# Second FFN cut into four groups with block steps in fourteen places, first queries projected ahead of the later values, sign changes tied to their places

## The chip, the core and the metric

The program runs on one NeuronCore of a Trainium2 chip. Its engines work side by side, each through its own list in order: TensorE (PE, the matrix engine; PEld is its loading of weights), VectorE (DVE), ScalarE (ACT), GpSimd (POOL) and SyncE (SP), which issues most of the transfers from device memory. PE writes into PSUM; DVE and ACT read it from there. The metric is the device time of one execution in microseconds (us), as the median of the runs. The times before were 1147.1, 1148.95 and 1351.8 us.

## The reference

Two trunk layers over 512 tokens of width 1024, batch 1. Layer 0 mixes by attention (with 256 context tokens), layer 1 by a Fourier transform and a linear map; both end with a gated feed-forward net (FFN) of width 2816 with a width-3 convolution. Every sub-layer stands between two RMS norms, with shift, scale and gate (adaLN) computed from the conditioning vector.

```python
for i in range(2):
    sh1, sc1, g1, sh2, sc2, g2 = split(silu(c) @ mod_w[i] + mod_b[i], 6)
    h = rms_norm(x, norm_g[i, 0]) * (1 + sc1) + sh1
    if i == 0:
        proj = h @ w_in                 # queries a, b, then keys and values a, b
        y = concat([global_attention(...), window_attention(...)]) @ w_out
    else:
        y = real(fft2(h.reshape(512, 4, 256), axes=(0, 2))) @ w_f
    x = x + g1 * rms_norm(y, norm_g[i, 1])
    h = rms_norm(x, norm_g[i, 2]) * (1 + sc2) + sh2
    u = h @ w_up                        # 1024 -> 2 x 2816
    u = up[:-2] * cw[0] + up[1:-1] * cw[1] + up[2:] * cw[2] + cb
    gate, val = split(u, 2)
    x = x + g2 * rms_norm((silu(gate) * val) @ w_down, norm_g[i, 3])
```

## The kernel before

All data stay transposed: 128 channels on the partitions, tokens along the row. An fp32 operand is split into a high part (fp32r) and the rest, and a product takes three matmuls: high by high (L98), one rest (L99) and the other (L100). For a weight, SP loads the raw fp32 tile (ring `raw`, three buffers), ACT casts the high part `wh`, DVE subtracts to get `wl` (both L121), and the pair stands in the ring `wpair` of five buffers.

An FFN runs over 22 chunks `fi` of 128 gate and 128 value channels. A plain up step takes 2 x 8 x 3 = 48 matmuls of 512 columns. A block step (`seven_products`; the chunks listed in `SEVEN`) computes the 2 x 2 blocks of the same product by seven block products: 7 x 4 x 3 = 84 matmuls of 256 columns. It needs four weight pairs of 1 MB in all instead of two, a second raw buffer filled by DVE sums (L1126, L1128, L1129), and two corrections of its outputs on DVE (L1168, L1171). After either step `conv` (ACT L1222, DVE L1223 and L1225, twice each) and `gated` (product L1236, split into a high and a low part, L121) follow.

The chunks are gathered in `GROUPS`, before (0 to 7), (8 to 13), (14 to 21). When the up steps of a group are through, its eight down tiles d = 0 to 7 follow: one raw tile each (512 KB for 8 chunks, 384 KB for 6), 3 matmuls per chunk, and from the second group on an addition to `yT` on DVE (L1343). The generator `gem` forms sums for the last adaLN vectors (raw loads of `mod_r`, L423 and L426 on DVE); `pump` advances a generator by one step. In the last group ACT loads a table early through `once` (L1358), so that the reciprocal square root of the norm (L186) finds it there.

In the attention part `project` runs for the groups of heads `kb` (keys), `vb` (values) and `qa` (queries), in that order, and the queries go through the norm on DVE, the rotation (to L773) and transposes on PE (L951). In the Fourier part `up_weights_dma` fetches the first pairs of the FFN without ACT casts or DVE rests: GpSimd's queue loads `xh`, ACT writes its negative into `xl` (L1093), and a second transfer adds the weight to `xl`. There, the loop over d = 0 to 7 multiplies by `w_f`; its weights are sums and differences (POOL and DVE), cast on ACT (L121) and split on DVE.

The order of instructions on each engine is set by the code's order and by a scheduler that sorts it with a planner's costs; each engine then runs its list strictly in order. The `later` and `held` marks shift single instructions in that list.

## Time and profile before

| | us |
|---|---|
| runs | 1147.1, 1148.95, 1351.8 (median 1148.95) |
| profiled execution, its time | 1146.93 |
| its span in the profile | 1145.2 |
| clock granted to PE, mean | 0.992 |
| attention start to end of layer 0, then Fourier part, FFN of layer 1 | 0 to about 690, 690 to 760, 760 to 1145 |

The profile lists, for one execution, each engine's busy time, the groups of instructions by source line, the transfers, and the chain of work that ended last. The table of stretches gives busy time within a stretch of the span; PEclk is the clock that PE was granted there, as a share of full speed. Stretches between 924.64 and 1075.02 us hold single up steps of layer 1 and serve as the price list below. Consecutive instructions on an engine overlap by some hundredths of a microsecond, so start times lie a little closer than the durations say.

### The profile page before, as it was taken

The numbers are of one execution on the slowest core, as the hardware profiler recorded it, in microseconds if no ns is written. First come the engines' busy times: TensorE is split into PE (matmuls) and PEld (weight loads), VectorE is DVE, ScalarE is ACT, GpSimd is POOL, SyncE is SP. The second block draws the span as 40 slices with busy tenths as digits, with TensorE's granted clock in tenths as the row PEclk, the third lists the DMA queues.
The fourth block names the chain that finished last, engine by engine and source line by source line (L and its number), as shares of the span: only waits on it lengthen the run. The fifth ranks groups of instructions, "written<-read, shape, count | busy, mean of one in ns | idle before, by whom it ended". The sixth has DMA issues, their size and how long they took to land.

```text
span 1145.2 us, 19120 instructions
## 1 busy us (share of the span) xinstructions
PE 1117.5 (98%) x7658; PEld 964.3 (84%) x7658; DVE 871.9 (76%) x1418; ACT 579.2 (51%) x1032; POOL 174.3 (15%) x180
## 2 busy tenths in 40 slices
PE   8999999999999999999999999999999999999996
PEld 5689988868898978987898898879887888899895
DVE  4678777765679976987999667878996498679745
ACT  4342356665665633552465545557743455256542
POOL 1136332421420000000000153510000000000012
PEclk9999999999999999999999999999999999999998
DMA  9576101075142355635534301920227223223212
GB/s 371 242 240 213 45 1 38 13 261 205 38 185 111 103 198 214 221 120 203 193 110 175 108 26 57 258 92 35 74 82 254 75 106 111 86 99 111 93 56 74
DMA packets 31745, 151.61 MB, mean 132 GB/s; under 512 B 3236, under 2 KB 7972, under 8 KB 19752
## 3 DMA queue, kind: packets, MB, share of 16 engines
q1 hardware_dynamic: 30504, 146.19, 36.0%
q0 software_dynamic: 1152, 4.19, 1.5%
q8 instruction: 60, 0.98, 0.3%
q14 instruction: 29, 0.24, 0.1%
HBM read 146.18 MB, written 4.19 MB: 131 GB/s over the span
## 4 chain that ended last, share of the span: by engine, by line
PE 89%; DVE 6%; ACT 4%; issue 1%; DMA 0%; POOL 0%; DVEq 0%; SPq 0%; ACTq 0%; POOLq 0%
PE mm L98 26%; PE mm L99 24%; PE mm L100 24%; PE PT L922 1%; ACT wh L121 1%; PE O L98 1%; PE gm L499 1%; PE gm L98 1%; PE O L99 1%; PE gm L100 1%; PE gm L99 1%; PE mm L174 1%; PE O L100 1%; PE mm L180 1%; DVE md_t L231 1%
## 5 line engine op out<-in xcount | busy, mean ns | idle before, releaser
L121 ACT CAST wh<-raw 128x1024 fp32r<-128x1024 f32 (+2 forms) x189 | 180.3, 966 | 186.6 <-PE mm L99 125.0
L121 DVE TENSOR_TENSOR wl<-raw,wh 128x1024 fp32r<-128x1024 f32 (+3 forms) x179 | 202.9, 1142 | 65.3 <-ACT wh L121 65.1
L98 PE MATMUL mm<-hh,wh 128*128 128x256 f32 (+2 forms) x652 | 221.0, 339 | 1.3 <-ACT yT L897 0.9
L99 PE MATMUL mm<-hl,wh 128*128 128x256 f32 (+2 forms) x652 | 218.2, 335 | 0.0
L100 PE MATMUL mm<-hh,wl 128*128 128x256 f32 (+2 forms) x652 | 217.9, 334 | 0.0
L273 POOL TENSOR_TENSOR gacc<-gacc,sq 128x256 f32<-128x256 f32 (+1 forms) x33 | 29.6, 897 | 717.6 <-ACT sq L271 716.9
L98 PEld LDWEIGHTS mm<-hh,wh 128*128 128x128 f32 x652 | 122.5, 188 | 18.6 <-ACT sq L1162 2.7
L100 PEld LDWEIGHTS mm<-hh,wl 128*128 128x128 f32 x652 | 122.6, 188 | 14.1
L99 PEld LDWEIGHTS mm<-hl,wh 128*128 128x128 f32 x652 | 122.6, 188 | 13.8
L98 PE MATMUL mm<-xh,wh 128*128 128x512 f32 (+1 forms) x368 | 131.6, 358 | 0.0
L99 PE MATMUL mm<-xl,wh 128*128 128x512 f32 (+1 forms) x368 | 131.1, 356 | 0.0
L100 PE MATMUL mm<-xh,wl 128*128 128x512 f32 (+1 forms) x368 | 130.1, 354 | 0.0
L98 PE MATMUL mm<-zh,wh 128*128 128x256 f32 x304 | 86.5, 285 | 0.0
L99 PE MATMUL mm<-zl,wh 128*128 128x256 f32 x304 | 84.3, 277 | 0.0
L100 PE MATMUL mm<-zh,wl 128*128 128x256 f32 x304 | 84.3, 277 | 0.0
L98 PEld LDWEIGHTS mm<-xh,wh 128*128 128x128 f32 x368 | 69.1, 188 | 12.8 <-issue 2.1
L99 PEld LDWEIGHTS mm<-xl,wh 128*128 128x128 f32 x368 | 69.1, 188 | 11.3 <-issue 0.4
L100 PEld LDWEIGHTS mm<-xh,wl 128*128 128x128 f32 x368 | 69.0, 188 | 11.1
L1222 ACT ACTIVATE cv<-mm,cols 128x512 f32<-128x512 f32 x64 | 49.7, 776 | 28.1 <-PE mm L100 25.0
L98 PEld LDWEIGHTS mm<-zh,wh 128*128 128x128 f32 x304 | 57.2, 188 | 3.6 <-ACT sq L1165 2.8
L1223 DVE SCALAR_TENSOR_TENSOR cv<-mm,cols,cv 128x511 f32<-128x511 f32 x64 | 47.5, 744 | 12.9 <-ACT cv L1222 12.4
L99 PEld LDWEIGHTS mm<-zl,wh 128*128 128x128 f32 x304 | 57.2, 188 | 0.0
(426 smaller groups left out, 2681.7 us busy)
## 6 DMA issues: line engine op xcount, KB each, us to landing
raw<-in_w_up SPq DMA_DIRECT2D x42, 1024.0 KB, 4.9
xT<-in_mod_r SPq DMA_DIRECT2D x20, 1024.0 KB, 4.9
raw<-in_w_down SPq DMA_DIRECT2D x32, 512.0 KB, 3.8
raw<-in_mod_p SPq DMA_DIRECT2D x8, 1024.0 KB, 5.0
raw<-in_w_in SPq DMA_DIRECT2D x6, 1024.0 KB, 8.0
raw<-in_w_down SPq DMA_DIRECT2D x16, 384.0 KB, 3.1
yT<-in_mod_r SPq DMA_DIRECT2D x10, 512.0 KB, 6.7
raw<-in_w_out SPq DMA_DIRECT2D x4, 1024.0 KB, 5.0
```

The lines of the kernel that those rows point to most:

```text
L98: i = PE.matmul(out, lhsT=ah, rhs=bh, start=start, stop=False, skip_group_check=skip)
L99: PE.matmul(out, lhsT=ah, rhs=bl, start=False, stop=False, skip_group_check=skip)
L100: return i, PE.matmul(out, lhsT=al, rhs=bh, start=False, stop=stop, skip_group_check=skip)
L121: i = S.copy(out=h, in_=src), eng.tensor_tensor(out=l, in0=src, in1=f(h), op=ALU.subtract)
L174: PE.matmul(ps[:32, :src.shape[1]], lhsT=ones32, rhs=src, start=True, stop=True)
L180: PE.matmul(ps[32 * j:32 * j + 32, :w], lhsT=ones32, rhs=sq[:, j * w:(j + 1) * w], start=first, stop=last)
L231: V.scalar_tensor_tensor(out=t, in0=src, scalar=am, in1=R, op0=ALU.mult, op1=ALU.mult)
L273: G.tensor_tensor(out=self.acc[:, sl], in0=self.acc[:, sl], in1=sq[:, sl], op=ALU.add)
L499: PE.matmul(ps[32 * q:32 * q + 32, :], lhsT=spad[:, k, :], rhs=w[:, q * T:(q + 1) * T], start=k == 0, stop=k == KC - 1)
L922: PE.transpose(out=pt[:, j * P:(j + 1) * P], in_=Ps[j][:, off:off + P], identity=ident)
L1222: S.activation(out=cv, in_=ps, func=AF.Identity, bias=bc, scale=wc[1])
L1223: V.scalar_tensor_tensor(out=cv[:, 1:], in0=ps[:, :T - 1], scalar=wc[0], in1=cv[:, 1:], op0=ALU.mult, op1=ALU.add)
```

## The change

1. The groups of layer 1 become (0 to 3), (4 to 9), (10 to 15), (16 to 21), and all of 8 to 21 are block steps (before, nine of them: 10, 13, 16, 19 and 21 were plain). The down tiles of a finished group no longer run in one piece: they are taken one or two at a time (four after 8 and 9) between the up steps of the next group, by the table `DOWN`. `gem` is advanced after down tiles 1, 4 and 7 of the middle groups, where it stood behind every tile of group 0. With the finer groups there are 32 down tiles for 24; the matmuls are as many.
2. The residual `xT` is stored to device memory (`away`, 2 MB) and its buffer holds gate pairs of chunks 0 to 3 and 10 to 13; it is loaded again in the last group, ahead of the weights of d = 6 and 7.
3. The early table load through `once` is removed in both layers. ACT's list now has the table load directly ahead of the reciprocal square root.
4. The attention projects `kb`, `qa`, `vb` instead of `kb`, `vb`, `qa`; the keys' and values' preparations for the first head stand behind the last `vb`, the inverse roots of the second half of the queries are put off by `later`, and the second job of `gate` has two buffers instead of all.
5. `up_weights_dma` issues its four sign changes one by one at d = 3, 4, 5 and 6 (before: all four by the pump at d = 4), each tied behind the last ACT instruction in the list. Two Fourier buffers move within `yT` for it.

```diff
-GROUPS = [(0, 8), (8, 6), (14, 8)]
+GROUPS = [[(0, 8), (8, 6), (14, 8)], [(0, 4), (4, 6), (10, 6), (16, 6)]]
...
-SEVEN = [(5, 6, 8, 10, 12, 14, 15, 17, 18, 20), (8, 9, 11, 12, 14, 15, 17, 18, 20)]
+SEVEN = [(5, 6, 8, 10, 12, 14, 15, 17, 18, 20), (8, 9, 10, 11, 12, 13, 14, 15, 16, 17, 18, 19, 20, 21)]
+DOWN = {8: 4, 9: 4, 10: 1, 11: 1, 12: 1, 13: 2, 14: 1, 15: 2, 16: 1, 17: 1, 18: 1, 19: 2, 20: 1, 21: 2}
...
-            for g, kind in enumerate(["kb", "vb", "qa"]):
+            for g, kind in ((0, "kb"), (2, "qa"), (1, "vb")):
...
-        for (wh, wl), src in ws:
-            S.activation(out=wl, in_=f(wh), func=AF.Copy, scale=-1.0)
-        yield
-        for (wh, wl), src in ws:
-            G.dma_start(out=wl, in_=src, accum_op=ALU.add)
+        for i, ((wh, wl), src) in enumerate(ws):
+            if i:
+                G.dma_start(out=ws[i - 1][0][1], in_=ws[i - 1][1], accum_op=ALU.add)
+            last = [j.name for j in nc.cur_bb.bb.instructions if j.engine == mybir.EngineType.Activation][-1]
+            j = S.activation(out=wl, in_=f(wh), func=AF.Copy, scale=-1.0)
+            tc.add_manual_dep(j.ins, last, mybir.DependencyInfo(
+                mybir.DependencyClass.NoSync, mybir.DependencyReason.DATA), reason="order")
+            yield
+        G.dma_start(out=wl, in_=src, accum_op=ALU.add)
...
-                gs["t"] = xp.pair([P, 2, T])
+                gs["t"] = places.pop(0) if l and (f0 == 0 or f0 == 10 and fi < 14) else xp.pair([P, 2, T])
...
+        def down_tiles(gi, nch, g_):
+            yield
+            for d in range(KC):
+                down_part(gi, down_weights(gi, nch, d, wpair), g_, d, [0, 1])
+
+                if gi and d % 3 == 1:
+                    pump(gem)
+                yield
...
+            SY.dma_start(out=away, in_=xT)
...
+                if l:
+                    pump(down, DOWN.get(fi, 0))
+            pump(down, 100)
+            if l and end:
+                xT = mk(cp, [P, KC, T], F32, "xT")
+                SY.dma_start(out=xT, in_=away)
...
+            if l and not end:
+                down = down_tiles(gi, nch, g_)
+                pump(down)
+                continue
...
-                S.activation(out=once, in_=g_[-1][0][:, 0:1].bitcast(F32), func=AF.Abs_reciprocal_sqrt, bias=eps, scale=0.0)
...
-            if d in (1, 4):
+            if d in (1, 3, 4, 5, 6):
                 pump(soon)
-            elif d == 6:
+            elif d == 7:
                 early = next(soon)
```

DVE's list in the FFN of layer 1, before, across a plain step and the block step behind it (rows of chunks 11 to 13; L121 with `wl` is the rest of a weight, with `xl` the low part of a gate, L1223 and L1225 the convolution):

```order
L1223 SCALAR_TENSOR_TENSOR cv_1404_9741<-mm_9716,cols_64,cv_1404_9741 128x511
L121 TENSOR_TENSOR wl_9799<-raw_9786,wh_9798 128x1024
L121 TENSOR_TENSOR xl_9579<-cv_1399_9702,xh_9578 128x512
L1225 SCALAR_TENSOR_TENSOR cv_1404_9741<-mm_9716,cols_64,cv_1404_9741 128x511
L121 TENSOR_TENSOR wl_9803<-raw_9784,wh_9802 128x1024
L1126 TENSOR_TENSOR raw_9914<-raw_9912 128x1024
L1223 SCALAR_TENSOR_TENSOR cv_1408_9774<-mm_9749,cols_64,cv_1408_9774 128x511
L1128 TENSOR_TENSOR raw_9914<-raw_9914,raw_9912 128x512
```

The same place after, from the last rest of a block step's weights (`wl_9756`) to the next block step's first (line numbers are two to ten higher; L1258 is the addition of a down tile, L425 and L428 are `gem`):

```order
L123 TENSOR_TENSOR wl_9756<-raw_9737,wh_9755 128x1024
L1235 SCALAR_TENSOR_TENSOR cv_1404_9699<-mm_9605,cols_64,cv_1404_9699 128x511
L1233 SCALAR_TENSOR_TENSOR cv_1405_9703<-mm_9606,ncw_8779,cv_1405_9703 128x511
L1258 TENSOR_TENSOR yT_68<-yT_68,mm_9717 128x512
L1235 SCALAR_TENSOR_TENSOR cv_1405_9703<-mm_9606,ncw_8779,cv_1405_9703 128x511
L123 TENSOR_TENSOR wl_9868<-raw_9865,wh_9867 128x768
L1246 TENSOR_TENSOR cv_1405_9703<-cv_1404_9699,cv_1405_9703 128x512
L425 TENSOR_SCALAR gacc_9891<-raw_9892,scol_78 128x1024
L123 TENSOR_TENSOR xT_8668<-cv_1405_9703,xT_8668 128x512
L428 SCALAR_TENSOR_TENSOR gacc_9891<-raw_9892,scol_78,gacc_9891 128x1024
L1135 TENSOR_TENSOR raw_9898<-raw_9896 128x1024
L123 TENSOR_TENSOR wl_9903<-raw_9896,wh_9902 128x512
```

The next step's sums (L1126) followed the last rest at once; now a down tile's addition and weights and, every third tile, two sums of `gem` stand between.

ACT's list in the Fourier part before, from its first sign change (L1093) past the casts of `w_f` for d = 2 and 3 (L121 with `gacc` and `yT`):

```order
L1093 ACTIVATE xl_7738<-xh_7737 128x1024
L1559 COPY qs_7724<-mm_7695 128x256
L1093 ACTIVATE xl_7740<-xh_7739 128x1024
L1563 COPY yT_68<-mm_7708 128x1
L1559 COPY qs_7778<-mm_7749 128x256
L1093 ACTIVATE xl_7742<-xh_7741 128x1024
L260 ACTIVATE acc_7729<-yT_68 128x512
L1563 COPY yT_68<-mm_7762 128x1
L121 CAST wh_7791<-gacc_7788 128x1024
```

And after (the sign change is L1101, the cast L123):

```order
L1597 COPY qs_7723<-mm_7694 128x256
L1601 COPY yT_68<-mm_7707 128x1
L1597 COPY qs_7777<-mm_7748 128x256
L262 ACTIVATE acc_7728<-yT_68 128x512
L123 CAST wh_7790<-gacc_7787 128x1024
L1601 COPY yT_68<-mm_7761 128x1
L123 CAST wh_7835<-yT_68 128x1024
L1101 ACTIVATE xl_7737<-xh_7736 128x1024
```

Three sign changes stood ahead of the cast for d = 2; now none does, and they follow singly among the later casts.

PE's list where the queries' transposes stand, before (`mm` here is a projection, `gm` the next):

```order
L98 MATMUL mm_1309<-wh_1214,hh_69 128x256
L99 MATMUL mm_1309<-wl_1215,hh_69 128x256
L100 MATMUL mm_1309<-wh_1214,hl_70 128x256
L951 MATMUL PT_1397<-con_66,yT_68 128x128 x2
L98 MATMUL gm_1404<-wh_1220,hh_69 128x256
```

And after, with the context's value projection (`ch`, `cl`) and the keys' transposes (L555) ahead of them:

```order
L101 MATMUL mm_1309<-wl_1192,ch_161 128x256
L102 MATMUL mm_1309<-wh_1191,cl_162 128x256
L452 MATMUL misc_1364<-con_66,sqx_160 128x128 x2
L555 MATMUL misc_1369<-con_66,K_82 128x128 x2
L555 MATMUL misc_1370<-con_66,K_82 128x128 x4
L956 MATMUL PT_1397<-con_66,yT_68 128x128 x4
L100 MATMUL gm_1404<-wh_1197,hh_69 128x256
```

The query projection is no longer the last one ahead of its own transposes; the values' projection lies between.

## The prediction

> **What bounds the kernel now.** I read the page's head and chain first, then busy time by stretch, then the groups of DVE, the transfers, and the three places where PE stands still.

> ```profile
> span 1145.2 us, 19120 instructions
> PE 1117.5 (98%) x7658; PEld 964.3 (84%) x7658; DVE 871.9 (76%) x1418; ACT 579.2 (51%) x1032; POOL 174.3 (15%) x180
> PE 89%; DVE 6%; ACT 4%; issue 1%; DMA 0%; POOL 0%; DVEq 0%; SPq 0%; ACTq 0%; POOLq 0%
> 903.93:924.64 20.71, 20.64 (x170) 19.90 (x168) 13.22 (x16) 12.25 (x20) 0.00 (x0) 1.00 0.31 110
> 924.64:935.84 11.20, 11.20 (x51) 9.01 (x49) 10.99 (x16) 6.47 (x10) 0.00 (x0) 1.00 0.05 18
> 935.84:956.40 20.56, 20.49 (x170) 19.81 (x168) 17.53 (x23) 13.23 (x22) 0.00 (x0) 1.00 0.33 109
> 1064.90:1075.02 10.12, 10.12 (x86) 9.91 (x84) 6.53 (x9) 6.21 (x10) 0.00 (x0) 1.00 0.41 134
> ```

> PE is busy 98% of the span and carries 89% of the chain, so only two things shorten the kernel: less PE work, or the 27.7 us in which PE stands. In the four stretches (length, then busy PE, weight loads, DVE, ACT, POOL, the granted clock, transfers) PE has no gap: two block steps in a row take 20.56 to 20.71 us (10.28 to 10.36 each), one plain step 11.20, a block step that stands alone 10.12.

> **The FFN of layer 1, PE's work.** Before: nine block steps and five plain ones for chunks 8 to 21, 9 x 10.3 + 5 x 11.20 = 148.7 us. After: fourteen block steps, each beside down tiles as the last stretch is, 14 x 10.12 = 141.7 us. That is 7.0 us less; priced as pairs (10.3) the saving is 4.5, and I keep both ends. The down tiles have as many matmuls as before: a tile of six chunks is 18 matmuls, and as 48 take 11.20 us it takes 4.2.

> **The same cycle on DVE.** These are the prices (count, busy us, mean ns, idle before):

> ```profile
> L121 DVE TENSOR_TENSOR wl<-raw,wh 128x1024 fp32r<-128x1024 f32 x21 | 25.6, 1218 | 11.5 <-ACT wh L121 11.5
> L1223 DVE SCALAR_TENSOR_TENSOR cv<-mm,cols,cv 128x511 f32<-128x511 f32 x9 | 6.7, 746 | 0.8 <-ACT cv L1222 0.6
> L1126 DVE TENSOR_TENSOR raw<-raw 128x1024 f32<-128x1024 f32 x4 | 4.9, 1218 | 0.0
> L121 DVE TENSOR_TENSOR xl<-cv,xh 128x512 fp32r<-128x512 f32 x6 | 4.1, 688 | 0.2
> L1236 DVE TENSOR_TENSOR cv<-cv,cv 128x512 f32<-128x512 f32 x6 | 4.1, 686 | 0.0
> L1168 DVE TENSOR_TENSOR mm<-mm,sq 128x512 f32<-128x512 f32 x5 | 3.5, 695 | 0.5 <-PE mm L100 0.5
> L1129 DVE TENSOR_TENSOR raw<-raw,raw 128x512 f32<-128x512 f32 x4 | 2.7, 685 | 0.0
> L1343 DVE TENSOR_TENSOR yT<-yT,mm 128x512 f32<-128x512 f32 x7 | 4.8, 686 | 9.4 <-PE mm L100 9.4
> L121 DVE TENSOR_TENSOR wl<-raw,wh 128x768 fp32r<-128x768 f32 x7 | 6.7, 952 | 2.3 <-ACT wh L121 2.3
> L426 DVE SCALAR_TENSOR_TENSOR gacc<-raw,scol,gacc 128x1024 f32<-128x1024 f32 x7 | 9.0, 1283 | 4.2 <-DMA raw<-in_mod_r 4.1
> L423 DVE TENSOR_SCALAR gacc<-raw,scol 128x1024 f32<-128x1024 f32 x1 | 0.8, 753 | 0.6 <-DMA raw<-in_mod_r 0.6
> 122.24 0.69 DVE L757 TENSOR_TENSOR sq<-mm,Rs 128x512 f32<-128x512 f32 x1
> 122.84 0.68 DVE L762 TENSOR_REDUCE qst<-sq 128x4 f32<-128x512 f32 x1
> raw<-in_w_up SPq DMA_DIRECT2D x42, 1024.0 KB, 4.9
> raw<-in_mod_r SPq DMA_DIRECT2D x4, 1024.0 KB, 6.4
> away<-xT SPq DMA_DIRECT2D x1, 2048.0 KB, 6.9
> xT<-away SPq DMA_DIRECT2D x1, 2048.0 KB, 7.7
> 771.41 32.76 SPq L130 DMA_DIRECT2D raw<-in_w_up  x2
> 811.67 0.67 DVE L121 TENSOR_TENSOR xl<-cv,xh 128x512 fp32r<-128x512 f32 x1
> ```

> A block step costs DVE three rests of 1.22 and one of half the size (as L1129, 0.69), one sum of 1.22, two of 0.69, two corrections of 0.70, four convolution steps of 0.74, a product of 0.69 and a low part of 0.69: 12.7 us. A down tile adds 0.69 + 0.95 = 1.64. The start times 122.24 and 122.84 lie 0.60 apart for a duration of 0.69, so about 0.08 of each is overlap: 17 instructions, 14.3 - 1.4 = 12.9 us of DVE against 10.12 + 4.2 = 14.3 us of PE. DVE keeps up with one tile per step, and with two it has 4 us to spare. With a `gem` advance of two sums (0.75 + 1.28, less the overlap 1.9) it needs 14.8: over by 0.5.

> The wait inside such a cycle costs more than its sum. `raw` has three buffers: the load of `mod_r` takes the one that the last rest of the step before gives back, about 2 us into that step by DVE's order, and lands 4.9 to 6.4 later, at some 7.5. DVE stands at L425 until then, with the next block step's sums and rests queued behind it. From there to the last rest DVE has 17 instructions (2.0 of `gem`, the low part 0.7, the weights 6.9, corrections 1.4, convolution 3.0, the tile's addition 0.7), 14.7 less 1.4 = 13.3: 20.8, which is 6.5 us into the next step. PE reaches the product that reads it after 30 of the step's 84 matmuls, 3.6 us in. So PE stands some 2.5 to 3 us; I take 2.5, since the clock of the load varies. That happens where one tile alone stands with `gem`, at steps 12 and 18; steps 14 and 16 have two tiles and 4 us of slack. Step 8, the first of the fourteen, has four pairs to prepare while PE spends only a plain step (11.20 in place of 14.3); counted the same way it is 2 us late. Sum 7.0 us (4 to 9).

> So this part nets 7.0 - 7.0 = 0 (from -5 to +5 by its own ends). Other edits here: eight more additions on DVE (8 x 0.69) stand in the cycles counted above. ACT's extra casts lie in a stretch where it is busy about 60%. The store of `xT` (6.9 us) only reads it and comes between the two loads that SP issued from 771.41 to 804.17; the residual is complete before the norm that the convolution needs, and the first low part of a gate, which would go into its buffer, is written at 811.67: cost 0, and up to 3 if the store leaves SP only with the second load. The reload (7.7 us) can start when the last middle tile is through; d = 6 then lands some 9 us into the last group and PE needs it after about 14: cost 0; with that cover gone, 2.

> **Fourier part.**

> ```profile
> 724.48 1.06 ACT L1093 ACTIVATE xl<-xh 128x1024 fp32r<-128x1024 f32 x1 [3.03 <-DMA xh<-in_w_up]
> 725.69 1.06 ACT L1093 ACTIVATE xl<-xh 128x1024 fp32r<-128x1024 f32 x1
> 727.17 1.06 ACT L1093 ACTIVATE xl<-xh 128x1024 fp32r<-128x1024 f32 x1
> 728.96 1.05 ACT L121 CAST wh<-gacc 128x1024 fp32r<-128x1024 f32 x1
> 728.06 0.28 PE L100 MATMUL mm<-A,wl 128*128 128x258 f32 x1
> 730.06 0.39 PE L98 MATMUL mm<-B,wh 128*128 128x256 f32 x1 [1.72 <-ACT wh L121]
> 731.00:734.40 3.40, 3.40 (x16) 3.36 (x16) 3.37 (x3) 1.71 (x3) 3.40 (x3) 0.50 1.06 219
> ```

> ACT waits 3.03 us for a transfer that nothing urgent needs, then negates three tiles ahead of the cast on which PE stands from 728.06 to 730.06. Right behind it PE runs 3.4 us at half clock (0.50), which loses 1.7 more. With no sign change ahead, the cast's next limits are its differences on POOL and DVE; I put it at 726.8 to 727.7 instead of 728.96. Most of the 1.8 us gap closes and the slow stretch with it: -3.0 (between -1.2, the gap less a third with the slow stretch staying, and -3.6, all of both). The sign changes cost the same 4 x 1.06 on ACT, one in each of four steps of the loop; the accumulating transfers end later, but the first products with them come only after the norm.

> [...]

> **Attention.**

> ```profile
> 125.92 0.69 DVE L773 TENSOR_TENSOR yT<-yT,sq 128x512 f32<-128x512 f32 x1
> 126.66 0.44 PE L951 MATMUL PT<-con,yT 128*128 128x128 f32 x2 [1.63 <-DVE yT L773]
> 142.66 1.19 DVE L163 TENSOR_SCALAR qtm<-qst 128x8 int32<-128x8 int32 x1
> 144.56 0.45 PE L100 MATMUL S<-kh,ql 128*128 128x384 f32 x1 [1.20 <-DVE ql L121]
> ```

> PE waits 1.6 us for the rotated queries, and 1.2 for a low part that stands on DVE behind the inverse root of queries not needed yet. With the values' projection between the queries and their transposes, the first goes; with the root put off, the second: -2.8. What is late next is DVE itself, with the second `gate` job on two buffers: a load that DVE waits for holds the norm behind it. I allow 0.3 for that: -2.5, between -2.8 and +1 (one such wait as long as the gap at 126.66 with the other gap staying away).

> **Table load.**

> ```profile
> 643.02 1.28 ACT L1358 ACT_TABLE_LOAD   x1
> 665.96 0.42 ACT L271 ACTIVATE sq<-yT 128x256 f32<-128x256 f32 x1 [2.41 <-DVE yT L1343]
> 666.98 0.31 ACT L186 ACTIVATE st_r<-misc,eps 128x64 f32<-128x64 f32 x1 [0.60 <-PE misc L180]
> ```

> The load was hidden at 643. Now it can begin when the last square ends at 666.38, and holds the root until 667.66 instead of 666.98: +0.7, up to 1.3 if it waits for the sums too. PE has few products to spare there. In layer 1 the first half's norm runs under the second half's matmuls: 0.

> **Sum.** 0 (FFN) - 3.0 - 2.5 + 0.7 = -4.8 on the profiled execution's 1146.93: 1142 us. The median of the runs, 1148.95, counts a disturbed one; the other two are 0.2 and 2.0 above the profiled time.

> **Rivals.** (a) DVE and the raw ring bind every cycle. A 1 MB load that lands after 6.4 us (the row of `mod_r`) instead of 4.9 takes 1.5, about what the single-tile cycles spare (14.3 - 12.9). If loads of `w_up` beside those of down tiles take longer than that, each further 1 us is lost in ten cycles, and if each gap brings the half clock of 731.00 it costs another 1.7. One microsecond late with no slow clock: +10, so 1152; with the slow clock in half of the cycles, 1160. Against it: DVE's 12.9 against 14.3, and transfers at only 0.41 of their time in a block step. It is slower than before from about 0.5 us late per cycle. (b) No new gaps: if the order hides the `gem` load and step 8's pairs, the FFN gives its whole 7.0, and the time is 1146.93 - 7.0 - 3.0 - 2.5 + 0.7 = 1135. For it: the slack of the two-tile cycles lets DVE run ahead. (c) The gains at attention and Fourier only shift: PE meets the next late operand there as it did before, and the FFN stays at 0: 1146.93 + 0.7 = 1147.6. For it: DVE's rows at 122.24 and 142.66 follow each other without a pause, so it is loaded there.

> **How the numbers follow.** Forecast, gains at both early places and new gaps that eat the FFN's saving (1138 to 1146): 0.55. (b), 1131 to 1138: 0.20. (c), 1146 to 1150: 0.13. (a), 1150 to 1165: 0.12. The range 1133 to 1151 leaves out about a quarter of (b) and most of (a), under 2 in 10. Two per cent, about what a measurement of this kernel can tell from no change, is 23 us: below 1126 or above 1172. No case sums to a gain of that size (all gains at their ends give 7.0 + 3.6 + 2.8 = 13.4), and (a) would need slow clocks in nearly all cycles. Faster 0.02, same 0.95, slower 0.03.

> **What would show it.** In the profile after: block steps of 10.1 us between 860 and 1080 with gaps of some 2.5 at steps 12 and 18 that DVE's rest releases, and DVE waiting for `mod_r` ahead of them; no gap at 728 and no half clock behind it; no gap at 126; a table load at about 666. I am wrong if gaps stand in every cycle (a), if steps 12 and 18 run through (b), or if the stretches before 160 and from 700 to 755 are as long as before (c).

## The result and the profile after

The changed kernel takes 1157.83 us (1156.45 to 1160.47) against 1148.31: a ratio of 1.0091, 95% interval 1.0078 to 1.0104. It is 10 us slower, outside the range of 1133 to 1151, where 1142 was forecast. For the kernel before, a fourth execution of 1147.66 us has joined the three shown above; the ratio leaves out the disturbed one of 1351.8 us. The first lines of its page:

```profile
span 1155.8 us, 19506 instructions
PE 1117.5 (97%) x7796; PEld 969.9 (84%) x7796; DVE 902.6 (78%) x1469; ACT 595.4 (52%) x1068; POOL 170.8 (15%) x180
PE 81%; DVE 11%; ACT 3%; POOL 2%; issue 2%; DMA 1%; POOLq 0%; DVEq 0%; SPq 0%; ACTq 0%
```

PE is busy for the same 1117.5 us and stands 38.3 us (1155.8 - 1117.5) instead of 27.7. It carries 81% of the chain instead of 89%, and DVE 11% instead of 6%.

To place the difference I cut the span at instructions that both kernels have, by their start times in the traces (us):

| stretch | before | after |
|---|---|---|
| start to the transposes of the first row sums | 13.7 | 12.2 |
| attention, to the last score product | 261.2 | 265.4 |
| rest of layer 0, to the first Fourier product | 420.4 | 421.5 |
| Fourier part, to the last product of its loop | 58.0 | 57.5 |
| norm and first up steps | 48.7 | 48.7 |
| FFN of layer 1, first full-width step to last down product | 330.7 | 338.0 |
| tail | 12.4 | 12.6 |

The first row differs from one execution to another (12.1 to 14.1 in all kernels here), whatever the change. The losses are 4.2 us in the attention and 7.3 in the FFN; the stretch with the table load is 1.1 longer. No instruction waits for the stored or reloaded residual, so this edit costs nothing, as forecast.

In the attention PE now stands longest at three places (start, duration, engine, line, operation, tiles, and in brackets the idle time before it and what ended it):

```profile
117.58 0.64 PE L442 MATMUL misc<-sqx,ones 128*32 128x256 f32 x8 [2.08 <-DVE qrs L166]
126.53 0.38 PE L100 MATMUL gm<-wh,hh 128*128 128x256 f32 x1 [1.83 <-DVE kl L123]
148.91 0.66 PE L927 MATMUL PT<-con,P 128*128 128x128 f32 x4 [1.26 <-POOL P L1011]
118.17:121.58 3.41, 3.41 (x20) 3.41 (x17) 1.80 (x11) 0.84 (x2) 0.00 (x0) 0.50 0.00 0
114.29 1.27 DVE L481 SCALAR_TENSOR_TENSOR sqx<-cT,scol,sqx 128x1024 f32<-128x1024 f32 x1
116.16 1.27 DVE L481 SCALAR_TENSOR_TENSOR sqx<-cT,scol,sqx 128x1024 f32<-128x1024 f32 x1
```

PE's sum over the gate job waits until DVE has taken in the job's last two tiles, at 116.16. The row names as releaser the small DVE instruction that comes behind it; the tile in the product, `sqx`, tells the cause. The next gap follows at 124.4 (2.0 us). It ends with the keys' low part `kl`, which DVE took up behind a weight's rest; the casts ahead of that were late, since ACT had waited for PE until 121.11. The third row is the gap that stood at 144.56 before: it has not gone, but moved from the scores to a transpose.

The gaps given in the text and in the table below are pauses between the starts of two products beyond their usual distance. They are 0.15 to 0.2 us longer than the idle time in brackets. In this stretch those over 0.3 us add up to 10.8 us, against 8.1 before. The fourth row is a stretch at half clock (0.50) behind the first gap, which loses 1.7 more; before, the attention has none. Together that is 4.4, about the 4.2 lost.

In the FFN the stretches of four steps, one without a gap and three with (length, busy PE, weight loads, DVE, ACT, POOL, granted clock, transfers):

```profile
934.00:948.60 14.60, 14.55 (x104) 13.36 (x103) 13.64 (x19) 8.36 (x14) 0.00 (x0) 1.00 0.40 124
1000.40:1017.30 16.90, 14.73 (x103) 13.36 (x102) 13.35 (x19) 9.13 (x14) 0.00 (x0) 1.00 0.23 85
1017.30:1032.40 15.10, 14.64 (x104) 13.24 (x104) 12.77 (x15) 6.37 (x12) 0.00 (x0) 1.00 0.46 167
1032.40:1054.10 21.70, 18.59 (x114) 16.31 (x113) 16.09 (x25) 10.58 (x17) 0.00 (x0) 0.84 0.19 68
```

Step 12 (the first row) runs through although the sums of `gem` stand ahead of it; step 16 loses 2.3 us, step 17 has a gap of 0.6, and step 18 loses 2.8 us and some 3 more at half clock, which lasts 6.8 us from 1036.36 (last row below) and makes 0.84 over the stretch. What PE and DVE waited for at steps 16 and 18:

```profile
1003.13 0.39 PE L102 MATMUL mm<-hh,wl 128*128 128x256 f32 x1 [2.11 <-DVE wl L123]
1036.86 0.58 PE L102 MATMUL mm<-hh,wl 128*128 128x256 f32 x1 [2.58 <-DVE wl L123]
1026.07 1.29 DVE L428 SCALAR_TENSOR_TENSOR gacc<-raw,scol,gacc 128x1024 f32<-128x1024 f32 x1 [2.05 <-DMA raw<-in_mod_r]
991.84 1.28 DVE L428 SCALAR_TENSOR_TENSOR gacc<-raw,scol,gacc 128x1024 f32<-128x1024 f32 x1
994.32 1.27 DVE L428 SCALAR_TENSOR_TENSOR gacc<-raw,scol,gacc 128x1024 f32<-128x1024 f32 x1
1036.36:1043.18 6.82, 5.85 (x25) 5.56 (x26) 5.57 (x8) 3.35 (x5) 0.00 (x0) 0.50 0.35 118
```

Both times PE stands for the last rest of a block step's weights. Ahead of step 18 DVE stood 2.05 us for the load of `mod_r`. Ahead of step 16 it did not wait for it; its two sums (2.5 us) simply stand in its list ahead of that step's weights.

### The profile page after: what moved, and what is told of

Same layout as the page of the kernel before. It is cut to its first block, busy times and chain, and to the rows that moved or that the text cites. A ratio compares the mean times of both kernels' runs of the same rounds, so it can differ in the third digit from the quotient of the medians.

```text
span 1155.8 us, 19506 instructions
## 1 busy us (share of the span) xinstructions
PE 1117.5 (97%) x7796; PEld 969.9 (84%) x7796; DVE 902.6 (78%) x1469; ACT 595.4 (52%) x1068; POOL 170.8 (15%) x180
## 3 DMA queue, kind: packets, MB, share of 16 engines
q0 software_dynamic: 1152, 4.19, 1.5%
## 4 chain that ended last, share of the span: by engine, by line
PE 81%; DVE 11%; ACT 3%; POOL 2%; issue 2%; DMA 1%; POOLq 0%; DVEq 0%; SPq 0%; ACTq 0%
PE mm L100 23%; PE mm L102 22%; PE mm L101 22%; DVE wl L123 2%; PE PT L927 2%; PE gm L100 1%; DVE md_t L300 1%; PE O L100 1%; PE gm L102 1%; PE gm L101 1%; PE O L101 1%; PE gm L504 1%; PE O L102 1%; DVE md_t L233 1%; PE mm L176 1%
## 5 line engine op out<-in xcount | busy, mean ns | idle before, releaser
L123 ACT CAST wh<-raw 128x1024 fp32r<-128x1024 f32 (+2 forms) x207 | 190.3, 933 | 154.8 <-PE mm L101 88.5
L123 DVE TENSOR_TENSOR wl<-raw,wh 128x1024 fp32r<-128x1024 f32 (+2 forms) x197 | 213.7, 1099 | 46.7 <-ACT wh L123 46.4
L102 PE MATMUL mm<-hh,wl 128*128 128x256 f32 (+1 forms) x632 | 204.2, 323 | 4.7 <-DVE wl L123 4.7
L100 PE MATMUL mm<-hh,wh 128*128 128x256 f32 (+1 forms) x632 | 207.2, 328 | 1.4 <-ACT yT L902 0.9
L101 PE MATMUL mm<-hl,wh 128*128 128x256 f32 (+1 forms) x632 | 203.7, 322 | 0.0
L100 PEld LDWEIGHTS mm<-hh,wh 128*128 128x128 f32 x632 | 119.3, 189 | 17.3 <-ACT sq L1171 4.8
L100 PE MATMUL mm<-zh,wh 128*128 128x256 f32 x384 | 109.9, 286 | 2.2 <-ACT sq L1169 1.3
L102 PE MATMUL mm<-zh,wl 128*128 128x256 f32 x384 | 107.4, 280 | 0.0
L100 PE MATMUL mm<-xh,wh 128*128 128x512 f32 (+1 forms) x302 | 107.3, 355 | 0.0
L101 PE MATMUL mm<-xl,wh 128*128 128x512 f32 (+1 forms) x302 | 106.7, 353 | 0.0
L102 PE MATMUL mm<-xh,wl 128*128 128x512 f32 (+1 forms) x302 | 106.2, 352 | 0.0
L100 PEld LDWEIGHTS mm<-zh,wh 128*128 128x128 f32 x384 | 73.0, 190 | 6.8 <-ACT sq L1174 3.8
L102 PEld LDWEIGHTS mm<-zh,wl 128*128 128x128 f32 x384 | 72.8, 190 | 0.4 <-DVE wl L123 0.3
L100 PEld LDWEIGHTS mm<-xh,wh 128*128 128x128 f32 x302 | 56.8, 188 | 9.9 <-issue 1.6
## 6 DMA issues: line engine op xcount, KB each, us to landing
raw<-in_w_up SPq DMA_DIRECT2D x42, 1024.0 KB, 4.9
xT<-in_mod_r SPq DMA_DIRECT2D x20, 1024.0 KB, 4.8
raw<-in_mod_p SPq DMA_DIRECT2D x8, 1024.0 KB, 4.9
raw<-in_w_in SPq DMA_DIRECT2D x6, 1024.0 KB, 8.0
raw<-in_w_out SPq DMA_DIRECT2D x4, 1024.0 KB, 4.9
```

What stands on the lines that cost most here:

```text
L100: i = PE.matmul(out, lhsT=ah, rhs=bh, start=start, stop=False, skip_group_check=skip)
L101: PE.matmul(out, lhsT=ah, rhs=bl, start=False, stop=False, skip_group_check=skip)
L102: return i, PE.matmul(out, lhsT=al, rhs=bh, start=False, stop=stop, skip_group_check=skip)
L123: i = S.copy(out=h, in_=src), eng.tensor_tensor(out=l, in0=src, in1=f(h), op=ALU.subtract)
```

## The experiments

Each part was first put alone into the kernel before.

**The attention part alone** (order `kb`, `qa`, `vb`, the later roots, two buffers for the second gate job).

> Only the new order of the attention's projections (kb, qa, vb), with its later inverse roots and the two buffers of the second gate job; the rest is the kernel before. Theory 1, from the trace of the changed kernel: PE now stands at about 115 us for the gate's sums on DVE (2.1 us) and at 124 us for the next weights (2.0 us); the time is 2.5 to 4.5 us above before. Rival: the order gains what the prediction said, and the delay in the trace has another source (a start that differs between executions): 2.5 us below before.

1.0029 (1.0016 to 1.0042): 3.3 us slower, with the same gaps at 115 and 124 us and the same short stretch at half clock. The attention is the loss, not a gain.

**Two buffers alone.** Only the gate's buffers change, with the old order of the projections:

```diff
-                ws[n] = places[n % len(places)]()
+                ws[n] = places[n % len(places) if n < KC else 3 + n % 2]()
...
-            load(n + len(places))
+            if n + len(places) < KC:
+                load(n + len(places))
+            for m in {3: (8,), 4: (9,)}.get(n, (n + 2,) if n >= KC else ()):
+                load(m)
```

> The kernel before with one thing of the attention part: the second gate job has two buffers instead of five; the projections keep their order kb, vb, qa. Theory 1, that the two buffers chain the loads and the gate's sum comes late on PE: PE stands for that sum where it did not, and the time is 1.5 to 4 us above before. Rival, that the order of the projections makes the gap at 115 us, by putting the queries' norm into DVE's list ahead of the sum: within 0.8 us of before and no gap at the sum.

1.0061 (1.0048 to 1.0075): 7 us slower. DVE's gate sums and PE's sum over them in this kernel:

```profile
107.30 2.61 DVE L479 SCALAR_TENSOR_TENSOR sqx<-cT,scol,sqx 128x1024 f32<-128x1024 f32 x2 [5.22 <-DMA cT<-in_mod_r]
112.31 1.28 DVE L479 SCALAR_TENSOR_TENSOR sqx<-cT,scol,sqx 128x1024 f32<-128x1024 f32 x1 [2.12 <-DMA cT<-in_mod_r]
115.09 1.28 DVE L479 SCALAR_TENSOR_TENSOR sqx<-cT,scol,sqx 128x1024 f32<-128x1024 f32 x1 [1.50 <-DMA cT<-in_mod_r]
116.53 1.08 PE L440 MATMUL misc<-sqx,ones 128*32 128x256 f32 x8 [6.91 <-DVE sqx L479]
94.24 2.82 SPq L465 DMA_DIRECT2D cT<-in_mod_r  x2
99.24 11.03 SPq L465 DMA_DIRECT2D cT<-in_mod_r  x4
cT<-in_mod_r SPq DMA_DIRECT2D x10, 512.0 KB, 4.9
116.53:122.26 5.73, 5.73 (x30) 4.92 (x31) 1.85 (x2) 0.37 (x1) 0.00 (x0) 0.50 0.52 183
```

And in the kernel before, with five buffers:

```profile
84.69 0.33 SPq L465 DMA_DIRECT2D yT<-in_mod_r  x1
100.43 0.33 SPq L465 DMA_DIRECT2D yT<-in_mod_r  x1
107.97 1.42 DVE L479 SCALAR_TENSOR_TENSOR sqx<-yT,scol,sqx 128x1024 f32<-128x1024 f32 x1 [1.28 <-DMA yT<-in_mod_r]
110.89 0.64 PE L440 MATMUL misc<-sqx,ones 128*32 128x256 f32 x8
```

The job has eight tiles. The first two are loaded early in both kernels (issued from 73 to 77 us). Of the other six the first is issued at 84.69 before, but only at 94.24 with two buffers, and the last at 109.94 instead of 100.43: here a load waits until the sum two tiles back has freed its buffer (the last one is issued at 109.94, and that sum ends at 109.91), and in this job it takes 5.1 us on average to land. From 94.24 to the end of the last sum at 116.37 pass 22.1 us, three rounds of two tiles. So the job's last sums move from 108 to 115 us, and PE stands 6.9 us for them, with half clock until 122.26 behind it (last row of the first list). The new order fills a part of this time with the queries and loses 3.3 instead of 7. The new order with all five buffers was not run, so whether the order alone gains stays open.

**The gate's sums earlier.** The attention part, with two advances per place beside the keys instead of beside the queries (`pump(gate, 2 if kind == "kb" else 1)`).

> The attention part alone, with the gate sums advanced twice per place beside the keys and not beside the queries. Theory 1, that DVE has the queries' norm and the gate's sums to do at the same time: the gap at 115 us goes and with it the late weights at 124: 3 to 5 us below the attention part alone, so 0 to 1.5 us below before. Rival, that two buffers for the second gate job make DVE wait for loads: DVE stands for transfers beside the keys, PE waits there instead, and the time is no better than the attention part alone.

1.0064 (1.0042 to 1.0087), worse than the attention part: the rival. PE's gaps are now 2.6 us at 91 and 3.0 at 114, and DVE again waits for loads into `cT` (1.28 and 1.60 us). But at the second gap the load is not the last to come:

```profile
115.62 1.28 DVE L479 SCALAR_TENSOR_TENSOR sqx<-cT,scol,sqx 128x1024 f32<-128x1024 f32 x1
112.00:116.00 4.00, 2.21 (x19) 2.00 (x17) 4.00 (x9) 0.00 (x0) 0.00 (x0) 1.00 0.02 6
```

The last tile had landed at 112.85, and DVE took it at 115.62; until then it was busy without a pause, with the queries' norm and rotation and a weight's rest. So two things delay the sum: the loads through two buffers, and DVE's list behind a load that came late.

**The Fourier part alone**, and the same without the moved buffers.

> Only the sign changes bound one by one, with the moved Fourier buffers in yT. Theory 1, from the trace of the changed kernel: the wait at 728 us goes, but the sum on POOL for d = 1 can no longer run at 706 us, runs beside DVE's rests instead and makes them 1.6 to 1.8 us long; PE stands there, half clock follows, and nothing is gained: within 0.8 us of before. Rival, the prediction: 3.0 us below before.

> Only the sign changes bound one by one; the Fourier buffers in yT stay where they were before. Theory A, that the moved buffers are what takes the gap at 707 us away and brings those at 720 us: the gap at 707 (1.7 us) stays, none at 720, and the gap at 728 is gone: 1 to 2 us below before and 1 to 2 us above the whole Fourier part. Theory B, that the bound sign changes do all of it: the same time as the whole Fourier part, 2.9 us below before.

The second kernel lacks the two hunks of the diff that touch `yT` in `fourier_load` and `fourier_weights`. The whole part gives 0.9972 (0.9962 to 0.9983), 3.2 us faster: the forecast held here, and my reading after the fact (nothing gained) fell. It is also a version that beats both kernels. Without the moved buffers it is 0.9985 (0.9976 to 0.9994), theory A. The moved buffers give and take. First the rests of the first two weights in the kernel with the whole part, and PE behind them; then POOL's sum for d = 1 in the kernel before, with DVE and PE around it, and the half clock behind that; last POOL's sums in the kernel with the whole part:

```profile
717.28 1.64 DVE L121 TENSOR_TENSOR wl<-gacc,wh 128x1024 fp32r<-128x1024 f32 x1
719.31 1.83 DVE L121 TENSOR_TENSOR wl<-yT,wh 128x1024 fp32r<-128x1024 f32 x1
721.20 0.39 PE L100 MATMUL mm<-B,wl 128*128 128x256 f32 x1 [0.61 <-DVE wl L121]
```

```profile
705.94 1.28 POOL L1500 TENSOR_TENSOR yT<-yT 128x512 f32<-128x512 f32 x1
705.91 1.60 DVE L356 SCALAR_TENSOR_TENSOR hl<-xT,der,hh 128x256 fp32r<-128x256 f32 x1
709.01 0.38 PE L98 MATMUL misc<-wh,hh 128*128 128x256 f32 x1 [1.56 <-DVE Z L121]
710.52:713.92 3.40, 3.40 (x17) 3.12 (x16) 2.24 (x8) 2.30 (x5) 0.00 (x0) 0.50 0.00 0
```

```profile
716.09 1.74 POOL L1504 TENSOR_TENSOR yT<-yT 128x512 f32<-128x512 f32 x1 [9.81 <-DVE mm L1483]
717.80 2.26 POOL L1504 TENSOR_TENSOR yT<-raw 128x512 f32<-128x512 f32 x1
```

Before, POOL's sum ran at 705.94 beside a DVE instruction that took 1.60 us instead of 0.48 (its like at 708.93), and PE stood 1.56. With the moved buffer POOL's two sums run at 716.09 and 717.80, beside two rests, which take 1.6 to 1.8 us instead of 1.2; PE stands 0.3 and 0.6 there and only 0.5 at the old place. In these rows a DVE instruction beside a sum on POOL is 0.4 to 1.1 us longer; what makes it so, no run shows.

The pauses themselves did not shrink: those over 0.3 us in the Fourier part add up to 4.4 us before and 5.2 with the whole part. What went is the half clock: before, it holds for two stretches of 3.4 us, at 710.52 and at 731.00, and with the whole part there is none. Over all kernels here the length of the Fourier part follows their number. With the old part it is 58.0 to 58.2 us with two such stretches (five kernels) and 59.5 to 59.9 with three (six kernels); with the new part 56.0 with none (six kernels) and 57.5 with one (the changed kernel). Without the moved buffers it is 57.2, with one.

**The FFN part alone**, and with the sums of `gem` moved. The kernels of this group have the FFN part and differ in where `pump(gem)` stands; four of them also have the Fourier part, none the attention part, and all keep the early table load. In `down_tiles`:

```diff
-                if gi and d % 3 == 1:
+                if gi and d in (4, 7):
+                if not gi and d % 2:
+                if gi == 1 and d in (1,):
+                if gi == 1 and d in (1, 4):
+                if gi == 0 and d in (2, 6) or gi == 1 and d in (1, 4):
                     pump(gem)
```

Each added line belongs to one kernel, in the order of the table below. The two that have `gi == 1` alone, and the one beside the plain steps, which has no such line, advance the rest in the loop over the steps:

```diff
+                if l and 4 <= fi < 8:
+                if l and fi in (5, 6, 7):
+                if l and fi in (6, 7):
+                    pump(gem)
                 if l:
                     pump(down, DOWN.get(fi, 0))
```

The last kernel has no advance in either place.

> Only the FFN of layer 1: four groups, fourteen block steps, down tiles and adaLN sums between them; the early table load stays. Theory 1: gaps of 2.3 and 2.7 us at steps 12 and 18, several of 0.6 to 0.8 and one stretch of half clock cost 14, the block steps save 7: 6.5 to 8 us above before. Rival, the prediction: 0, since the rest of the loss would come from work that the other parts push into this stretch.

> As the FFN part alone, but the adaLN sums are advanced only after down tiles 4 and 7 of the middle groups, where two tiles stand in one cycle, not after tile 1. Theory 1, that the load of mod_r and DVE's wait for it make the gaps at steps 12 and 18: both gaps and the half clock go, 6 to 7 us below the FFN part alone, so within 1.5 us of before. Rival, that DVE and the raw ring bind every cycle: the sums only move the gaps, and the time stays 4 us or more above before.

> The FFN part alone, with the adaLN sums advanced after the plain steps 4 to 7 and no longer between block steps. Theory 1, that the sums in DVE's list hold back the weights of the block step behind them (with or without a wait for the load): no gap of 2 us is left at any block step; gaps of 0.6 to 0.8 may stay; 5 to 7 us below the FFN part alone, so 1149 to 1152. Rival, that DVE and the ring of three raw buffers bind the cycles: gaps of 2 us stay in at least two steps and the time is 4 us or more above before.

> The Fourier part and the FFN part, without the attention part and with the early table load kept; the adaLN sums are advanced beside the first group's down tiles (after tiles 1, 3, 5, 7), where four tiles of 2.8 us of PE stand in one cycle. Theory 1, that where the sums stand decides, and that the five changed steps save 0.9 each: the FFN runs 4 us shorter than before, with no gap over 1 us, and the Fourier part 2 to 3: 1141 to 1143. Rival, that the sums only move the wait, as from the middle groups to the plain steps: a gap of 2 us or more beside the first down tiles, 1144 to 1147.

> The Fourier part and the FFN part, with three advances of the adaLN sums after the plain steps 5, 6 and 7 and the last after tile 1 of the second group, where the changed kernel showed no gap; no attention part, early table load kept. Theory 1, that only the place of the sums stands in the way: no gap over 1 us in the FFN, which runs 4 us shorter than before, and with the Fourier part 1141 to 1143. Rival, that wherever the sums and the tiles stand, the smaller gaps add up to what the block steps save: the FFN within 1.5 us of before, 1145 to 1147.

> The same with two advances after the plain steps 6 and 7 and two after tiles 1 and 4 of the second group. Theory 1: as the kernel with three advances beside plain steps, within 1 us of it, 1141 to 1143. Rival: with two advances between block steps gaps return, 1144 to 1148.

> The Fourier part and the FFN part; the adaLN sums one at a time at four places: after tiles 2 and 6 of the first group and tiles 1 and 4 of the second, each in another cycle; no attention part, early table load kept. Theory 1, that only the place of the sums stands in the way: no gap over 1 us, the FFN 3 to 4.5 us shorter than before, with the Fourier part 1141 to 1143. Theory 2, that the sums take a raw buffer from the weights wherever they stand, and the interleaving itself has small gaps: the FFN no shorter than before, 1145 to 1149.

> The FFN part alone, with no advance of the adaLN sums among the steps: all four stand in one piece ahead of the last group, where PE must wait for them, so the whole time says nothing; the stretch from the first full-width step to the last block step does. Theory 1: that stretch has no gaps and is 5 to 8 us shorter than in the FFN part alone, with 10.3 us a block step. Theory 2: gaps of 0.4 to 0.8 at block steps stay, 3 us or more in all, and the stretch is at most 4 us shorter.

| kernel (sums of `gem` after) | ratio, 95% interval | FFN stretch, us (before 330.7) | gaps at steps over 0.3 us |
|---|---|---|---|
| FFN part alone (tiles 1, 4, 7) | 1.0068, 1.0051 to 1.0085 | 340.1 | 2.2 at 16, 2.8 at 18, nine of 0.3 to 0.8 |
| tiles 4 and 7 | 1.0047, 1.0032 to 1.0062 | 336.6 | 1.3 at 9, 1.7 at 16, 2.3 at 20, small ones |
| plain steps 4 to 7 | 1.0023, 1.0014 to 1.0033 | 332.5 | 3.9 at a plain step, none at a block step |
| first group's tiles, with Fourier part | 1.0068, 1.0055 to 1.0082 | 342.6 | seven of 0.65 to 1.3 at steps 8 to 10, many of 0.4 |
| plain 5 to 7, tile 1, with Fourier part | 1.0032, 1.0019 to 1.0044 | 337.7 | 3.9 at a plain step, ten of 0.3 to 0.6 |
| plain 6 and 7, tiles 1 and 4, with Fourier part | 1.0064, 1.0052 to 1.0077 | 341.2 | 5.4 at a plain step, many of 0.4 |
| four cycles, one each, with Fourier part | 1.0024, 1.0015 to 1.0033 | 335.8 | none over 0.8, nineteen of 0.4 to 0.75 |
| ahead of the last group | 1.0022, 1.0012 to 1.0032 | 334.2 | 0.8 and 1.3 at steps 8 and 9, then none; 2.5 and 1.5 in the last group |

No placement brings the FFN below 330.7. In my expectations theory 1 was right at single places and wrong on the sum: with the sums beside the plain steps all fourteen block steps run without a gap, and one plain step loses 3.9 us; spread one to a cycle, no gap exceeds 0.8 us, and nineteen small ones remain. The last kernel tells most of the cause, since it has no sums in the stretch. Its steps 11, 12, 13 and 17:

```profile
918.62:932.94 14.32, 14.32 (x103) 13.22 (x102) 12.84 (x18) 8.32 (x14) 0.00 (x0) 1.00 0.29 93
932.94:947.57 14.63, 14.63 (x105) 13.54 (x104) 13.08 (x18) 8.66 (x14) 0.00 (x0) 1.00 0.29 104
947.57:966.32 18.75, 18.75 (x122) 16.73 (x121) 17.04 (x24) 10.44 (x17) 0.00 (x0) 1.00 0.40 134
1014.28:1028.75 14.47, 14.47 (x104) 13.35 (x103) 13.00 (x18) 8.47 (x14) 0.00 (x0) 1.00 0.31 102
```

PE is busy without a pause (the first two numbers of each row agree), with DVE at 13.0 of 14.5 us. From the first full-width step to the last block step this kernel takes 283.7 us against 296.9 for the FFN part alone: 13.2 less, more than either theory said. So the interleaving as such has no gaps after step 9, and the large gaps at steps 16, 18 and 20 come with the sums.

The small gaps (0.3 to 0.75 us) are of another kind. They end with a copy or a cast by ACT, where the first products of a down tile stand inside the block step in PE's list. This one is from the kernel with one sum in each of four cycles:

```profile
1017.41 0.39 PE L100 MATMUL mm<-zh,wh 128*128 128x256 f32 x1 [0.23 <-ACT sq L1166]
```

They also stand far behind the sums: in the kernel with plain 5 to 7 and tile 1 the last sum runs at 926 us, and the small gaps stand from 987 to 1087. The kernel with the sums beside plain steps 4 to 7, and the last one from step 10 on, have none; there PE's list takes block steps and tiles as wholes. Moving the sums thus changed the scheduler's order as well, and why it did is shown by no run. The Fourier part is not the reason, since the changed kernel and the FFN part alone have nearly the same gaps (9.5 and 10.0 us in all).

The saving can be read from a sum: 330.7 us, less 4.5 for five steps at 10.3 instead of 11.2, plus the pauses over 0.3 us, plus 1.7 for each 3.4 us at half clock. For the plain steps 4 to 7 this gives 330.7 - 4.5 + 4.3 + 1.7 = 332.2 (measured 332.5), and for the last kernel 330.7 - 4.5 + 6.5 + 1.7 = 334.4 (measured 334.2). It holds within 1.2 us for the other kernels too, but for the one with the first group's tiles (339.7 against 342.6), where the rest stays open.

For the plain steps' gap, PE waits for a rest on DVE as well:

```profile
825.97 0.80 PE L102 MATMUL mm<-hh,wl 128*128 128x512 f32 x1 [3.77 <-DVE wl L123]
824.70 1.21 DVE L123 TENSOR_TENSOR wl<-raw,wh 128x1024 fp32r<-128x1024 f32 x1
```

DVE is busy without a pause from 803 to 828 us there, and the rest stands behind convolution steps. The sums themselves run only after it, at 829.36, so they do not hold it up directly; why the list came out in this order, no run shows.

**Fewer block steps, and no interleaving.** The FFN part with the old nine block steps (sums beside the first group's tiles), and the kernel before with fourteen block steps in its old groups; both change only the second list of `SEVEN`.

> The FFN part alone with the sums beside the first group's tiles, but with the nine block steps of before; early table load kept, no Fourier and no attention part. It separates the interleaving from the five more block steps. Theory 1: the interleaving alone saves nothing, since PE did not wait in this stretch before: within 1 us of before, and the FFN 4 to 5 us longer than with fourteen block steps. Rival, that the interleaving costs PE time by itself (gaps where a down tile's weights are late): 2 us or more above before.

> The kernel before with all fourteen steps as block steps, but the old groups, so the down tiles still run in one piece. If DVE's 12.9 us for a block step bind where no down tile stands beside it, PE waits some 2.6 us in most of the steps that follow one another: 10 to 25 us above before. Rival, that the buffers filled ahead cover it: the five steps save 0.9 each, 4 us below before.

Nine interleaved steps: 1.0063 (1.0049 to 1.0077), FFN stretch 339.0; its gaps (up to 1.7 us, 6.8 in all) stand only at steps 8 to 10, beside the sums, so this run tells the placement and not the interleaving. Fourteen steps without interleaving: 1.0103 (1.0087 to 1.0120), 343.5, with gaps of 1.0 to 2.2 where three and more block steps follow one another. That is 12 us slower, not 4 faster. The 12.9 us in my expectation was the price with a down tile; without one it is 12.7 less 15 overlaps of 0.08, an estimate of 11.5. Six and eight block steps in a row took 11.4 us a step, and DVE was busy nearly throughout:

```profile
915.00:960.00 45.00, 40.90 (x317) 38.90 (x316) 44.36 (x59) 27.12 (x46) 0.00 (x0) 0.96 0.23 80
```

So DVE binds there against 10.3 us on PE, and tiles in between are needed.

**The table load** (only the line with `once` removed), **and the later roots** (the kernel with the sums beside the first group's tiles, plus `with later(200 * qi):`).

> Only the early table load through once is left out, in both layers; nothing else changes. The prediction's term: the load begins after the last square of layer 0 and holds the root by 0.7 us, up to 1.3 where it waits for the sums too; nothing in layer 1: 0.7 to 1.3 us above before. Rival: the chain from the root to the first products of layer 1 is covered by products that PE has, so the time is the same within 0.3 us.

> As the kernel with the sums beside the first group's tiles, and of the attention part only the inverse roots of the second half of the queries put off. Theory 1, that these roots on DVE make the gap at 143 us (1.2 us): that gap goes, 1 to 1.5 us less. Rival, that DVE's list is full there and the next operand is late instead: the same time within 0.5 us.

The load alone: 1.0018 (1.0009 to 1.0027), about 2 us (1.0 to 3.1). ACT in this kernel:

```profile
666.66 1.28 ACT L186 ACT_TABLE_LOAD   x1
667.95 0.31 ACT L186 ACTIVATE st_r<-misc,eps 128x64 f32<-128x64 f32 x1
```

The root starts at 667.95, 1.3 us after the load began, where before it followed the sums; the rest of layer 0 is 421.8 us, against 420.4 to 420.8 in the kernels with the early load: 1.0 to 1.4 longer. The rows show 1.28 us for the load and the next instruction right behind it. The later roots: 1.0075 against 1.0068 without them, the same. The gap at 143 us has gone from the scores and stands at a transpose, 1.4 us long: the rival.

## Why the prediction was wrong

The four parts alone add up within their intervals: 0.9972, 1.0029, 1.0068 and 1.0018 give 1.0087 together, against 1.0091 measured. So no large effect between the parts is seen, and each step can be judged by its own run.

- **Attention: -2.5 forecast, +3.3 measured.** The step that failed is "I allow 0.3 for that": the second gate job on two buffers. I named the right object and priced it without following its loads. Six of its tiles pass through the two buffers in three rounds of 7.4 us, and the first of these loads leaves 9.5 us later than before. Alone this costs 7 us; with the new order a gap of 2.2, the gap of 2.0 behind it and a stretch at half clock are left. The gap at 126.66 did go, as forecast. The gap at 144.56 did not: it stands at a transpose, 1.5 us long, and with the later roots alone it is 1.4. The end of +1 was a slip as well, since its own condition gives -2.8 + 1.6 = -1.2.
- **FFN: 0 forecast, +7.8 measured.** Three terms failed. The block step's price: I took 10.12 us from the one that stood alone; interleaved ones take 14.3 to 14.6 with a tile of 4.2, so 10.3, the pairs' price, and the saving is 4.5 instead of 7.0. The gaps: step 18 came as described (2.8 for 2.5, with DVE waiting for `mod_r`), step 12 not at all, step 8 0.8 for 2, and step 16, which I had excluded because of its two tiles, 2.3. Counting the cycle's sum did not protect it, since DVE's list has the sums ahead of the weights. The half clock behind the gaps, which I had put at nothing in this part, as an assumption that no run shows: some 3 us behind step 18. This and the small gaps were nearest to rival (a), which I gave 0.12. Its trigger was not the one I described: `w_up` loads landed in 4.9 us as before. The large gaps come with the sums, and the cause of the small ones stays open. The range of this part, -5 to +5, was a slip: a saving of 4.5 to 7.0 against gaps of 4 to 9 gives -3 to +4.5.
- **Fourier: -3.0 forecast, -3.2 measured alone (-4.4 to -2.0).** The number was right, the mechanism only in part, and so close a hit is partly luck. The gap at 730.06 shrank from 1.9 to 0.5 us, and the half clock behind it went. But new pauses made up for what closed, and the gain is two stretches at half clock, of which I had named one. The other stood behind the gap at 709, which shrank from 1.7 to 0.6 when POOL's sum moved away from it; I had not priced that.
- **Table load: +0.7 forecast, up to 1.3; 1.0 to 1.4 in the stretch, about 2 in the runs.** Right in sign, a little small.

Rival (a) came nearest to the outcome, in sum and in its place on DVE, and the range that left most of it out was too narrow.

## What to carry to other kernels

Follow the loads through the ring: when a change takes buffers away, price the chain (buffer freed, load issued, landed, consumed) as a rate and set it beside the rate of the consumer, since an engine waiting in order for one late tile holds up all that is listed behind it (with two buffers DVE stood 5.22, 2.12 and 1.50 us for loads, and PE 6.91 us for the sums). A cycle whose sum of work fits can still stall, when side work stands ahead of the weights in the list of the fullest engine (at step 16 DVE was busy for 13.35 of 16.90 us, and PE stood 2.11); ask for each operand when its turn in the list comes, not only whether there is time. And take the price of a step from several instances beside the neighbours that it will have: the cheapest one was the exception here (10.12 us against 10.3).

## What the runs showed of the hardware

Half clock stood behind gaps of 0.6 us and less, and not each time. In the changed kernel the stretch from 720 to 760 us ran at a mean of 0.96 after gaps of 0.3 and 0.6 us; the kernel with the Fourier part alone has the same gaps there and ran at 1.00:

```profile
720.00:760.00 40.00, 36.91 (x288) 31.83 (x285) 31.30 (x45) 21.89 (x43) 24.51 (x20) 0.96 0.77 227
```

```profile
720.00:760.00 40.00, 36.58 (x292) 30.13 (x291) 32.57 (x53) 21.46 (x44) 21.10 (x19) 1.00 0.77 224
```

```profile
722.33:725.74 3.41, 2.75 (x15) 2.02 (x15) 3.41 (x8) 1.05 (x3) 3.41 (x5) 1.00 0.20 55
```

PE was busy for 2.75 of the 3.41 us ahead of the half clock here. Why equal gaps end differently, these two cases do not show. So a single profiled execution is uncertain by 1.7 us per such place, as the 58.0 to 59.9 us of the unchanged Fourier part show, which is as much as several of the terms that were argued about.
